# Far scores of the dilated heads read from copies sorted by residue

## The chip, the cores and the metric

The kernel runs on one core of a Trainium2 chip. The metric is the device time of one execution in microseconds (us). The kernel before takes 2331.02 us, the median of three runs (2330.0 to 2331.39).

## The reference, cut to what matters

The program is a trunk of two layers over 1024 positions and 1024 channels. Each layer projects its input into four groups of heads (Fourier mixing, grouped-query attention, a convolution module, dilated attention), joins them by an output projection, and then applies a two-matrix MLP; each half ends in a layer norm. What matters here is the dilated group, four heads of 64 channels:

```python
DIL_CONFIGS = ((128, 1), (512, 4), (2048, 16))      # window, dilation
def dilated_branch(q, k, v, dil, n, rel_bias):
    L = S // dil
    def to_res(t):                                   # positions sorted by their residue modulo dil
        return t.reshape(B, L, dil, H, hd).transpose(0, 2, 1, 3, 4).reshape(B * dil, L, H, hd)
    qr, kr, vr = to_res(q), to_res(k), to_res(v)
    ...
    s = jnp.einsum('bnqhd,bnkhd->bnhqk', qb, kw) * (hd ** -0.5)
    logits = jnp.where(valid, s + bias, NEG)         # |distance| <= n, T5 relative bias
    ...
```

Each query meets its neighbours at distance 1, those of its own residue modulo 4, and those of its own residue modulo 16. The branches are merged by their softmax denominators.

## The kernel before, in words

All matmuls run in a 32-bit format that keeps the upper part of a float, so values stand as a high and a low part; `split` (L168, L169) makes them, the high part on ScalarE and the difference on VectorE or GpSimd. `T` is one resident tile of 128 partitions x 8 rows x 2 parts x 1024 columns. It holds the layer's transposed activations and, during attention, pieces of other things. While attention runs, rows 0, 1, 4 and 5 hold the results of the Fourier and convolution groups, row 2 and the first half of row 3 hold the two `edge` tiles of the near branch (L629), row 6 takes the merged result of the first pair of dilated heads and row 7 that of the second pair, at its end. The second half of row 3 takes its first result near the end of attention.

`attention` handles 12 units: for each dilated head (4 to 7) a near unit and a far unit (class `Dilated`), then four dense heads (class `Dense`). A near unit is the branch of dilation 1; a far unit covers the branches of dilation 4 and 16 together, with one bias that counts both. Queries `qs` (high part in the upper, low part in the lower 64 partitions) and keys `kh`, `kl` (the same part twice) are loaded once for each head and used by its two units. Each of these tiles has two buffers, so the next head is loaded while this one runs.

A dilated unit has four steps. A step computes two score tiles of 128 queries x 256 keys, each as two matmuls, one with `kh` and one with `kl` (L823, L824): four matmuls per step. In a near step queries and keys are neighbours in memory. In a far step `i` queries and keys are those of residue `i` modulo 4, read at a stride of four elements:

```python
kk, q = slice(HD + i, HD + S, 4), me.q[:, 512 * qi + i:512 * qi + 512:4]
```

VectorE adds the bias and takes the row maximum (L834), ScalarE takes the exponential and its sum (L835). Seven steps later (`LAG`) TensorE transposes the probabilities (`turn`, L843), they are split, and two steps after that (`VLAG`) `values` multiplies by the values (L864); `join` (L677, L678) copies and adds the two halves of the result. `finish` and `merge` combine the near and the far unit of a pair of heads, by way of a round trip of the denominators through device memory (L890).

All of this is written into a table `todo` of step numbers, and the functions are called in the order of that table. Between the steps, sixteen pieces of the output projection for the other two groups (`others`, 12 matmuls each) are called. The order of the instructions on each engine is then set by a planner, which simulates the program with its own costs and may move instructions; the semaphores are made from what each instruction reads and writes. All loads and stores are issued by SP from one queue (L141); the two zero pads of the key tiles are written by GpSimd (L642, L643).

Of the kernel before, what the change touches and what calls it, by code (L numbers as in the profile page):

```python
# [15 lines left out]
F32 = mybir.dt.float32  # L16
# [6 lines left out]
P = 128  # L23
S = 1024
# [5 lines left out]
HD = 64  # L30
# [78 lines left out]
class Trunk:  # L109
# [513 lines left out]
    def attention(self, l, Wo):  # L623
        nc, tc = self.nc, self.tc
        g, v = nc.gpsimd, nc.vector
        with ExitStack() as c:
# [5 lines left out]
            for e in edge:  # L632
                for i in (1, 4):
                    v.memset(e[:, :, i].bitcast(F32), 0.0)
            pairs = {}

            def load_k(src, pad):
# [23 lines left out]
            def f4():  # L661
                return sm.tile([P, S], F32, tag="f4", name="f4", bufs=7)

            def s2():
                return self.sp.tile([P, S], F32, tag="s", name="s", bufs=2)
# [23 lines left out]
            class Dense:  # L689
# [22 lines left out]
                def scores(me, gr, kp):  # L712
                    t, n = 2 * gr + kp // 2, kp % 2
                    if n == 0:
                        me.s = s2()
                    s = me.s
                    q = me.q[:, t * P:(t + 1) * P]
                    nn = slice(n * 512, n * 512 + 512)
                    nc.tensor.matmul(s[:, nn], q, me.k[0][:, nn], start=True, stop=False)
                    nc.tensor.matmul(s[:, nn], q, me.k[1][:, nn], start=False, stop=True)  # L720
                    if n == 0:
                        return
                    pr = f4()
                    m = sm.tile([P, 2], F32, tag="m", name="m", bufs=4)
                    v.tensor_reduce(m[:, 0:1], s, AX.X, OP.max, negate=True)
                    nc.scalar.activation(pr, s, AF.Exp, bias=m[:, 0:1], scale=1.0, accum_out=m[:, 1:2])
                    v.reciprocal(me.rd[:, t, me.h % 2:me.h % 2 + 1], m[:, 1:2])
                    me.prob[t] = pr
# [34 lines left out]
            class Dilated:  # L763
# [5 lines left out]
                def load(me):  # L769
# [11 lines left out]
                    else:  # L781
                        me.st = pairs[me.near, me.h // 2].st

                def load_b(me):
                    b0 = self.bs[me.h - 4]

                    def skew(off, *dims):
                        return bass.AP(b0.tensor, b0.offset + off + P - 1, [[RL - 1, P], *dims])

                    if me.near:  # L790
                        me.b = sm.tile([P, 3, 256], F32, tag="ba", name="ba")
                        self.dma(me.b, skew(0, [0, 3], [1, 256]))
                        g.memset(me.b[:, 0, 0:HD], NEG)
                        g.memset(me.b[:, 2, 256 - HD:], NEG)
                    else:
                        me.b = sb.tile([P, 384], F32, tag="bb", name="bb")
                        self.dma(me.b, skew(LA, [1, 384]))
# [15 lines left out]
                def scores(me, i):  # L813
                    if i % 2 == 0:
                        me.s, me.p = s2(), f4()
                    sl = [slice((i % 2) * 512 + qi * 256, (i % 2) * 512 + qi * 256 + 256) for qi in range(2)]
                    for qi in range(2):
                        t = 2 * i + qi
                        if me.near:
                            kk, q = slice(t * P, t * P + 256), me.q[:, t * P:(t + 1) * P]  # L820
                        else:
                            kk, q = slice(HD + i, HD + S, 4), me.q[:, 512 * qi + i:512 * qi + 512:4]
                        nc.tensor.matmul(me.s[:, sl[qi]], q, me.k[0][:, kk], start=True, stop=False)  # L823
                        nc.tensor.matmul(me.s[:, sl[qi]], q, me.k[1][:, kk], start=False, stop=True)  # L824
                    for qi in range(2):
                        t = 2 * i + qi
                        pr = me.p[:, sl[qi]]
                        if me.near:
                            b = me.b[:, 0 if t == 0 else 2 if t == NT - 1 else 1]
                            st = me.st[:, t, :, me.h % 2]  # L830
                        else:
                            b = me.b[:, P * (1 - qi):P * (1 - qi) + 256]
                            st = me.st[:, 4 * qi + i, :, me.h % 2]
                        v.tensor_tensor_reduce(pr, me.s[:, sl[qi]], b, -1.0, 3e38, OP.add, OP.min, st[:, 0:1])  # L834
                        nc.scalar.activation(pr, pr, AF.Exp, bias=st[:, 0:1], scale=-1.0, accum_out=st[:, 1:2])  # L835
                    me.prob[i] = me.p[:, (i % 2) * 512:(i % 2) * 512 + 512].rearrange("p (q k n) -> p q k n", q=2, k=2)
# [76 lines left out]
            units = [Dilated(h, near) for h in range(4, 8) for near in (True, False)]  # L913
# [7 lines left out]
            first = {}  # L921
# [4 lines left out]
            def at(i, f, *args):  # L926
                todo.setdefault(i, []).append((f, args))
# [5 lines left out]
            for n, u in enumerate(units):  # L933
                hn = heads.index(u.h)
                at(0 if hn < 2 else begin[heads[hn - 1]], u.load)
                if isinstance(u, Dilated):
                    at(0 if n < 2 else first[units[n - 1]], u.load_b)
                at(0 if n < 2 else first[units[n - 1]] + LAG + VLAG + 1, u.load_v)
                last = first[u] + len(u.steps) + LAG + VLAG - 1
                at(last + 1, u.finish)  # L940
                if isinstance(u, Dilated):
                    at(last + 4, u.merge)
# [677 lines left out]
```

## Time and profile before

| | us |
|---|---|
| median of three runs | 2331.02 |
| the profiled execution | 2328.44 |
| its span, first to last instruction | 2326.3 |
| TensorE busy | 2217.1 (95%) |
| VectorE busy | 1776.1 (76%) |
| ScalarE busy | 1077.1 (46%) |
| GpSimd busy | 793.3 (34%) |

Times inside the trace count from the start of the span. A group of the profile is one line of the program on one engine with its operation and the shapes of its tiles; "idle before" is the time in which the engine stood in front of these instructions, and the arrow names what ended it. Matmuls overlap, so the distance of their starts tells what one costs, not its duration. `PEld` is the loading of the stationary operand (the queries, in the scores).

### The profile page before, as it was taken

How to read it: one execution, taken by the hardware profiler on the slowest of the kernel's cores; microseconds unless marked ns; L12 is line 12 of the kernel's file. 1: busy time of each engine (PE TensorE's matmuls, PEld its weight loads, DVE VectorE, ACT ScalarE, POOL GpSimd, SP SyncE). 2: the span in 40 equal slices, each digit the busy share in tenths (PEclk: the TensorE clock that was granted, in tenths of full speed). 3: DMA queues.
4: the chain of work that ended last, by engine and by line, in shares of the span. 5: the costliest groups of instructions: out<-in, count | busy, mean ns of one | idle time of the engine just before them, and what ended most of it. 6: DMA issues, size and time to landing. Idle time of an engine off the chain costs nothing. (4 is left out here: it accounts for less than half of the span.)

```text
span 2326.3 us, 31019 instructions
## 1 busy us (share of the span) xinstructions
PE 2217.1 (95%) x11212; PEld 1869.2 (80%) x11212; DVE 1776.1 (76%) x2500; ACT 1077.1 (46%) x1851; POOL 793.3 (34%) x540
## 2 busy tenths in 40 slices
PE   7999899998999999999989999999899999999997
PEld 6888887976778887888788798788677788788886
DVE  7687667968776777778957966788787767776699
ACT  3343767845333344333333446677443333443333
POOL 2361203016332233435514702110262333354353
PEclk9999999999999999999999999999999999999999
DMA  8444673043344467644223539621343444765433
GB/s 312 127 124 149 190 197 117 19 154 116 137 160 162 159 223 261 205 142 134 98 92 98 153 114 260 171 83 58 125 147 132 165 163 158 276 217 175 160 100 109
DMA packets 222950, 357.44 MB, mean 154 GB/s; under 512 B 21416, under 2 KB 100716, under 8 KB 221708
## 3 DMA queue, kind: packets, MB, share of 16 engines
q1 hardware_dynamic: 222796, 355.45, 47.1%
q8 instruction: 89, 1.46, 0.3%
q14 instruction: 65, 0.53, 0.1%
HBM read 244.44 MB, written 115.15 MB: 155 GB/s over the span
## 5 line engine op out<-in xcount | busy, mean ns | idle before, releaser
L174 PE MATMUL x<-T,w 128*128 128x512 f32 x1088 | 425.5, 393 | 12.2 <-DVE x L1441 4.7
L176 PE MATMUL x<-T,w 128*128 128x512 f32 x1088 | 425.0, 391 | 4.0 <-POOL w L169 2.6
L175 PE MATMUL x<-T,w 128*128 128x512 f32 x1088 | 426.2, 392 | 2.8 <-DVE T L169 2.8
L174 PEld LDWEIGHTS x<-T,w 128*128 128x128 f32 x1088 | 205.3, 189 | 60.8 <-issue 9.7
L176 PEld LDWEIGHTS x<-T,w 128*128 128x128 f32 x1088 | 205.6, 189 | 49.4 <-POOL w L169 3.4
L175 PEld LDWEIGHTS x<-T,w 128*128 128x128 f32 x1088 | 205.7, 189 | 46.7 <-DVE T L169 4.2
L1420 POOL TENSOR_TENSOR w<-w 128x512 fp32r<-128x512 f32 x76 | 147.5, 1961 | 225.1 <-ACT w L1418 225.1
L169 POOL TENSOR_TENSOR w<-raw,w 128x512 fp32r<-128x512 f32 x96 | 138.3, 1466 | 236.7 <-ACT w L168 221.4
L169 POOL TENSOR_TENSOR w<-s,w 128x512 fp32r<-128x512 f32 x68 | 104.3, 1544 | 246.2 <-ACT w L168 165.9
L174 PE MATMUL x<-E,w 128*128 128x512 f32 x384 | 150.6, 392 | 5.9 <-ACT h L1269 4.5
L176 PE MATMUL x<-E,w 128*128 128x512 f32 x384 | 150.1, 392 | 2.0 <-POOL w L169 1.8
L175 PE MATMUL x<-E,w 128*128 128x512 f32 x384 | 150.0, 391 | 0.0
L174 PE MATMUL s<-w,T 128*128 128x256 f32 (+1 forms) x432 | 137.0, 318 | 5.8 <-ACT T L168 5.4
L176 PE MATMUL s<-w,T 128*128 128x256 f32 (+1 forms) x432 | 135.0, 313 | 1.6 <-POOL T L169 1.2
L175 PE MATMUL s<-w,T 128*128 128x256 f32 (+1 forms) x432 | 134.8, 313 | 1.3 <-POOL w L169 1.3
L169 POOL TENSOR_TENSOR w<-rw,w 128x512 fp32r<-128x512 f32 x60 | 93.4, 1573 | 122.5 <-ACT w L168 122.5
L1047 DVE TENSOR_TENSOR s<-rw 128x512 f32<-128x512 f32 x62 | 53.4, 861 | 104.0 <-DMA rw<-in_w_ff_dram 103.7
L1418 ACT CAST w<-w 128x2048 fp32r<-128x2048 f32 x38 | 72.7, 1912 | 129.4 <-DMA w<-h_scratch 122.4
L174 PE MATMUL x<-T 128*128 128x512 f32 x320 | 126.1, 394 | 0.0
L175 PE MATMUL x<-T 128*128 128x512 f32 x320 | 125.5, 392 | 0.0
L176 PE MATMUL x<-T 128*128 128x512 f32 x320 | 125.4, 392 | 0.0
L456 DVE SCALAR_TENSOR_TENSOR o<-hp,cvT,o 128x1024 f32<-128x1024 f32 x88 | 113.3, 1287 | 2.4
(378 smaller groups left out, 5796.5 us busy)
## 6 DMA issues: line engine op xcount, KB each, us to landing
h_scratch<-h SPq DMA_DIRECT2D x224, 256.0 KB, 2.5
w<-h_scratch SPq DMA_DIRECT2D x38, 1024.0 KB, 5.4
rw<-in_w_ff_dram SPq DMA_DIRECT2D x64, 512.0 KB, 5.5
b<-in_w_ff_dram SPq DMA_DIRECT2D x24, 1024.0 KB, 5.5
raw<-x_scratch SPq DMA_DIRECT2D x72, 256.0 KB, 4.7
T<-h_scratch SPq DMA_DIRECT2D x18, 1024.0 KB, 5.3
raw<-in_w_in_dram SPq DMA_DIRECT2D x64, 256.0 KB, 3.5
rw<-in_w_ff_dram SPq DMA_DIRECT2D x10, 1024.0 KB, 5.3
```

Of the source, the lines that this page charges most:

```text
L169: (lo_eng or self.nc.vector).tensor_tensor(lo, src, hi.bitcast(F32), OP.subtract)
L174: mm(out, l[0], r[0], start=first, stop=False, skip_group_check=more)
L175: mm(out, l[0], r[1], start=False, stop=False, skip_group_check=more)
L176: mm(out, l[1], r[0], start=False, stop=last, skip_group_check=more)
L456: v.scalar_tensor_tensor(o, hp[:, m, k:k + S], cvT[:, m, k:k + 1], o, OP.mult, OP.add)
L1047: eng.tensor_tensor(quad(out), x, y, op)
L1418: nc.scalar.copy(A[:, :, 0], f32)
L1420: nc.gpsimd.tensor_tensor(A[:, j, 1], f32[:, j], A[:, j, 0].bitcast(F32), OP.subtract)
```

## The change

For each far unit a new function copies the head's queries and keys into rows of `T`, sorted by residue: `qr` is the second half of row 3 (1024 columns), `kr` is row 7, its two halves for the two parts of the keys. VectorE copies the queries, ScalarE the two parts of the keys. The copies are called at the step at which the near unit of the same head begins, ahead of its scores. The far scores then read 256 neighbouring columns of `kr` and 128 neighbouring columns of `qr`. There is one `kr` and one `qr` for all heads. The near scores read what they read before.

```diff
+            kr = self.T[:, 7]
+            qr = self.T[:, 2:4].rearrange("p k q n -> p (k q n)")[:, 24 * P:32 * P]
             pairs = {}
...
+                def by_residue(me):
+                    for copy, dst, x in ((v.tensor_copy, qr, me.q), (nc.scalar.copy, kr[:, 0], me.k[0][:, HD:HD + S]),
+                                         (nc.scalar.copy, kr[:, 1], me.k[1][:, HD:HD + S])):
+                        copy(dst.rearrange("p (r j) -> p r j", r=4),
+                             x.bitcast(F32).rearrange("p (j r) -> p r j", r=4))
+
...
                         if me.near:
-                            kk, q = slice(t * P, t * P + 256), me.q[:, t * P:(t + 1) * P]
+                            k, q = [x[:, t * P:t * P + 256] for x in me.k], me.q[:, t * P:(t + 1) * P]
                         else:
-                            kk, q = slice(HD + i, HD + S, 4), me.q[:, 512 * qi + i:512 * qi + 512:4]
-                        nc.tensor.matmul(me.s[:, sl[qi]], q, me.k[0][:, kk], start=True, stop=False)
-                        nc.tensor.matmul(me.s[:, sl[qi]], q, me.k[1][:, kk], start=False, stop=True)
+                            c = slice(256 * i, 256 * i + 256)
+                            k, q = [kr[:, x, c] for x in (0, 1)], qr[:, 256 * i + P * qi:256 * i + P * qi + P]
+                        nc.tensor.matmul(me.s[:, sl[qi]], q, k[0], start=True, stop=False)
+                        nc.tensor.matmul(me.s[:, sl[qi]], q, k[1], start=False, stop=True)
...
                     at(0 if n < 2 else first[units[n - 1]], u.load_b)
+                    if not u.near:
+                        at(first[units[n - 1]], u.by_residue)
```

## Rows read from the trace of the kernel before

**Rows 1.** The page, part 1: busy us, share of the span, instructions.
```profile
PE 2217.1 (95%) x11212; PEld 1869.2 (80%) x11212; DVE 1776.1 (76%) x2500; ACT 1077.1 (46%) x1851; POOL 793.3 (34%) x540
```

**Rows 2.** The windows view: both stages, their densest 30 us, 10 us of dense heads.
```profile
core 0: us, PE busy (x) PEld busy (x) DVE busy (x) ACT busy (x) POOL busy (x), PEclk, DMA share, GB/s
257.00:334.00 77.00, 71.22 (x384) 64.25 (x385) 46.18 (x180) 49.38 (x166) 6.70 (x25) 0.93 0.78 219
1404.00:1484.00 80.00, 73.90 (x415) 66.17 (x416) 54.11 (x195) 55.81 (x181) 6.76 (x26) 1.00 0.85 238
270.00:300.00 30.00, 29.23 (x163) 27.21 (x164) 20.93 (x87) 24.85 (x89) 3.67 (x16) 0.94 0.90 263
1420.00:1450.00 30.00, 29.89 (x170) 27.34 (x171) 22.21 (x85) 23.43 (x82) 2.93 (x15) 1.00 0.94 272
400.00:410.00 10.00, 10.00 (x73) 9.03 (x72) 9.76 (x17) 9.66 (x20) 1.29 (x1) 1.00 0.00 0
```

**Rows 3.** Time line of TensorE, layer 1: start, duration, line (us).
```profile
1440.76 0.28 PE L823 MATMUL s<-kh,qs 128*128 128x256 f32 x1
...
1441.23 0.28 PE L823 MATMUL s<-kh,qs 128*128 128x256 f32 x1
...
1442.98 0.36 PE L823 MATMUL s<-kh,qs 128*128 128x256 f32 x1
...
1443.53 0.49 PE L823 MATMUL s<-kh,qs 128*128 128x256 f32 x1
1443.84 0.42 PE L824 MATMUL s<-kl,qs 128*128 128x256 f32 x1
...
1444.55 0.66 PE L864 MATMUL o<-pT,vs 128*128 128x256 f32 x4
...
1445.40 0.58 PE L823 MATMUL s<-kh,qs 128*128 128x256 f32 x1
...
1446.51 0.42 PE L174 MATMUL tr<-w,T 128*128 128x512 f32 x1
```

**Rows 4.** Line 823 alone, near and far together: ns min/median/max.
```profile
L823 PEld LDWEIGHTS s<-kh,qs x128: 186/308/337, 257.1 to 1480.1; 128*128 128x128 f32 x128
```

**Rows 5.** Groups by form (ScalarE, VectorE), and line 907 alone (ns min/median/max).
```profile
L168 ACT CAST T<-d 128x1024 fp32r<-128x1024 f32 x16 | 16.8, 1051 | 63.7 <-DVE d L1471 42.0 <-PE x L176 21.7
L168 ACT CAST T<-b 128x2048 fp32r<-128x2048 f32 x30 | 57.2, 1908 | 81.6 <-PE x L176 78.1 <-DMA rw<-in_w_ff_dram 3.5
L598 ACT COPY u<-s 128x512 f32<-128x512 f32 x6 | 6.7, 1111 | 2.5 <-DVE T L169 1.5 <-PE s L176 1.0
L577 ACT COPY u<-s 128x512 f32<-128x512 f32 x3 | 1.8, 585 | 2.7 <-PE s L176 2.7
L169 DVE TENSOR_TENSOR T<-s,T 128x1024 fp32r<-128x1024 f32 x2 | 2.4, 1209 | 0.0
L907 DVE TENSOR_TENSOR y<-y,tr x12: 676/866/1082, 349.1 to 1540.9; 128x512 f32<-128x512 f32 x12
```

**Rows 6.** Time line of ScalarE: the first exponential of each layer.
```profile
261.76 0.51 ACT L835 ACTIVATE f<-f,std 128x256 f32<-128x256 f32 x1 [5.56 <-DVE std L834]
...
1407.85 0.51 ACT L835 ACTIVATE f<-f,std 128x256 f32<-128x256 f32 x1 [1.50 <-DVE std L834]
```

**Rows 7.** Time line of TensorE: the first dilated score of layer 0.
```profile
257.16 0.36 PE L823 MATMUL s<-kh,qs 128*128 128x256 f32 x1 [3.31 <-DMA kh<-k_scratch]
```

**Rows 8.** Waits, us in total, times, longest: the first three in layer 0, the others in layer 1.
```profile
POOL kh L642 <- PE s L823: 15.7, 2, 12.8
...
DVE w L890 <- DMA std<-merge_scratch: 5.1, 1, 5.1
...
SPq L141 <- PE s L824: 7.9, 3, 3.6
...
DVE w L890 <- DMA std<-merge_scratch: 3.4, 1, 3.4
...
SPq L141 <- PE s L824: 7.6, 4, 4.5
```

## The prediction

> **What bounds the kernel now.** The page comes first: TensorE is busy for 95% of the span, VectorE for 76%, ScalarE for 46% [rows 1]. These are averages, and the change touches only the stage in which the four dilated heads of a layer make their scores, so I cut that stage out with the windows view. It lasts from the first dilated score to the last one, 77 us in layer 0 (257 to 334) and 80 us in layer 1 (1404 to 1484). In it TensorE is busy for 71.2 and 73.9 us, ScalarE for 49.4 and 55.8, VectorE for 46.2 and 54.1, and the DMA engines carry a share of 0.78 and 0.85. In its densest 30 us TensorE is full (29.2 and 29.9), ScalarE is at 24.9 and 23.4, and the DMA share is 0.90 and 0.94 [rows 2]. So TensorE sets the pace here, with three others close behind it: what it is relieved of becomes time only as far as the others can follow.
>
> Then the matmuls themselves, in the time line of TensorE. A burst is the four matmuls of one score step. In a near burst the starts lie 0.12 us apart (four from 1440.76 to 1441.23); in a far burst, whose operands are read at a stride of four elements, 0.24 us apart (three from 1443.84 to 1444.55) [rows 3]. Its weight loads are longer too: the lines of the scores hold loads from 186 ns up to 337 ns, and the median over near and far is 308 ns [rows 4]. Both kinds have one shape and read the same tiles, so the stride alone is the difference, and copies without a stride should run like near bursts. That the change fails to do what it says is hardly possible.
>
> **What goes from TensorE.** Bursts are compared at the same place. Behind transposes a near burst holds the engine from 1442.98 to 1443.53, 0.55 us, a far one from 1445.40 to 1446.51, 1.11 us; behind other scores a near one takes 0.47 us (1440.76 to 1441.23) and a far one 1.02 us (1443.53 to 1444.55) [rows 3]. The gains are 0.56 and 0.55; between two far bursts the saving is four times 0.12, or 0.48. I take 0.53. There are 4 steps x 4 heads x 2 layers = 32 far bursts: 32 x 0.53 = 17.0 us, 8.5 in each layer (bounds 15.4 and 17.9). All of it lies on the engine that is full.
>
> **What ScalarE gets.** Two copies of 128x1024 per head, 16 in all, each reading every fourth element. No row shows ScalarE reading SBUF at a stride. From below: a 128x1024 cast with plain operands takes 1051 ns, and a stride will not make it shorter, so nothing below that. From above: a 128x512 copy from PSUM that *writes* at this stride takes 1111 ns, the plain one into the same tile 585 [rows 5]. That is 1.03 ns more for each element, so 1051 + 1024 x 1.03 = 2.1 us. I take the second kind, with the doubling that TensorE shows: the cast of 2048 elements takes 857 ns more than that of 1024, so 0.84 ns per element, and 1024 elements at twice that are 1908 ns. So 1.9 us a copy, 15.2 us per layer.
>
> The Trainium skill, page "SBUF — State Buffer", section Specifications, says that SBUF has lines of 16 bytes and that full bandwidth takes at least two hits in a line. A stride of four fp32 elements makes one hit per line; the far bursts at half rate agree. It speaks against this change, since the copies read the same way; by the rule they cost the 1.9 us, without it 1.05 us, and my forecast and my first rival differ in just this.
>
> Of these copies some are free. Head 4's come when ScalarE is idle: in layer 0 it waits 5.56 us for the first VectorE result, more than both copies, and in layer 1 1.50 us [rows 6]; the keys are there about then, since the first score itself waited for them until 257.16 [rows 7]. If that cover were gone it would cost 3.8 us a layer. What is left inside the stage is 6 x 1.9 = 11.4 us in layer 0 and, with some 1.1 us of head 4, 12.5 us in layer 1.
>
> **What VectorE gets.** One copy per head, 4 a layer. Nearest are the strided multiplies of the merge, at most 1082 ns against at least 676 for the plain ones of the same shape: 406 ns on 512 elements, or 0.81 us on 1024. A plain 128x1024 operation takes 1209 ns [rows 5]. So 2.0 us at the top; from below I allow half of the plain one, 0.6 us, since that reads two operands and the copy one. I take 2.0, 8 us a layer: 54.1 + 8 is 62.1 us in layer 1, below TensorE and ScalarE there. Cost: nothing, hidden beside TensorE's work; without that cover it would be 2 us for each of 6 head starts.
>
> **What the moves cost and give.** The copies of the next head overwrite rows that the far scores of this head read, so they wait for its last far burst, and they must end before the next far burst, 4 near steps later. In ScalarE's queue the casts of the transposes, the exponentials and the PSUM copies of the join stand behind them, and TensorE waits for the casts and joins to free PSUM. The order is the planner's, whose picture of the copies I do not know. In return the key tiles come free four steps earlier: SP waited 7.9 and 7.6 us for the last far scores before it could issue the next loads, and POOL 15.7 us in layer 0 [rows 8]. I count this at nothing, since TensorE waited for no key after each layer's first; gains up to 2 us are possible.
>
> **The sum.** How far can the stage shrink when ScalarE must also get through? It works for 49.4 + 11.4 = 60.8 us in layer 0 and 55.8 + 12.5 = 68.3 in layer 1. In its densest stretch here it was occupied 0.83 of the time (24.85 of 30); in the dense heads it reached 0.97 [rows 2]. I choose 0.87, near the former, since its queue is fed by the same mixture. Then the stage needs 60.8 / 0.87 = 69.9 us in layer 0, 7.1 less than 77, and 68.3 / 0.87 = 78.5 in layer 1, 1.5 less than 80; TensorE's 8.5 would have allowed more in both. Together -8.6 us. One wait takes some back: VectorE's first merge operation waited 5.1 us (3.4 in layer 1) for a round trip through memory [rows 8], which does not shrink with the work around it. About 2.5 far bursts lie between its issue and its use, 1.3 us, in each layer, so +2.6. The total is -6.0 us. The stages behind simply start earlier. The profiled execution took 2328.4 us (its span is 2326.3), so it would be 2322.4; the median of the runs shown is 2.6 us above the profiled one, so I forecast 2325.0 us.
>
> **Rivals.**
> *ScalarE reads a stride for free.* For it: TensorE takes an element every 0.46 ns (0.118 us for 256) and strided every 0.93, while ScalarE with 0.84 ns is slower than that anyway. Against it: the strided write of 1111 ns [rows 5]. The copies then add 6 x 1.05 = 6.3 us; at 0.87 ScalarE needs 64.0 and 71.4 us, TensorE 68.5 and 71.5, so TensorE binds and all is kept but the merge's wait: -17.0 + 2.6 = -14.4, 2316.6 us.
>
> *No gain.* ScalarE gets no more than the 0.83 of now: 73.3 us in layer 0 (-3.7) and 82.3 in layer 1 (+2.3), with the merge +1.2 in all; the key tiles' earlier release gives about that back. 2331 us.
>
> *Slower: a head start that TensorE stands through.* The two copies hold ScalarE's queue for 3.8 us, waiting as well for the last far burst, at each of the 6 head starts inside the stage. PSUM for transposes then stays full and TensorE stands. It decides from the point where a standstill is over 17.0 / 6 = 2.8 us; at the whole 3.8 the sum is 6 x 3.8 - 17.0 = +5.8, 2336.8 us. For it: ScalarE's queue is in order and already 0.83 full. Against it: seven steps of lag lie between scores and transposes, and the planner has matmuls of the output product to fill with.
>
> **How the numbers follow.** Forecast 0.40, free stride 0.20, no gain 0.18, slower 0.22. The measurement can tell 0.2% (4.7 us) from no change. Faster by more: most of the forecast (0.32), all of the free stride (0.20), 0.01 of no gain, 0.53. Slower by more: most of the last rival with a little of the others, 0.23. The rest, 0.24, is within. The range goes from 2314, where TensorE's 17 us are all kept, to 2337, the standstill; the forecast's own range is 2320 to 2328.
>
> **What would show it.** Far bursts with starts 0.12 us apart and weight loads near 186 ns (step 1). ScalarE's copies at 1.9 us; at 1.05 the first rival holds. VectorE's at 1 to 2 us. The stage in the windows view at some 70 and 78 us, with ScalarE above 0.85 of it. TensorE's waits at head starts on ScalarE's casts: short in the forecast, 3 us and more in the last rival. SP's and POOL's waits for far scores gone. I am wrong if the far bursts keep their spacing, or if the stage stays at 77 and 80 us while ScalarE is under 0.8.

## The result, and the profile after

The changed kernel takes 2349.57 us, the median of four runs (2344.19 to 2351.88), against 2330.51 for the kernel before, now the median of four runs as well: a ratio of 1.0086, with a 95% interval from 1.0064 to 1.0108. It is 19 us slower, and above the upper end of the forecast's range, 2337. Its profiled execution took 2344.19 us, 15.8 more than that of before, with a span of 2342.4.

The page, part 1, and then the changed far scores and the copies, each line alone (ns min/median/max, first and last start in us):

```profile
PE 2217.3 (95%) x11212; PEld 1863.6 (80%) x11212; DVE 1781.6 (76%) x2508; ACT 1106.0 (47%) x1867; POOL 795.2 (34%) x540
```

```profile
L834 PEld LDWEIGHTS s<-T x64: 186/188/337, 267.4 to 1496.8; 128*128 128x128 f32 x64
...
L791 DVE CAST T<-qs x8: 1073/1109/2124, 254.6 to 1473.3; 128x1024 fp32r<-128x1024 f32 x8
L791 ACT CAST T<-kl x8: 2012/2050/2093, 259.2 to 1475.2; 128x1024 fp32r<-128x1024 f32 x8
```

The weight loads of the far scores fall to a median of 188 ns, where near and far together had 308 [rows 4], and TensorE is as busy as before all the same [rows 1]. Now the stages, in the windows view. The first two rows answer to [rows 2]; the last two are cut from the layer's first dilated score to its first dense score, which moves from kernel to kernel:

```profile
core 0: us, PE busy (x) PEld busy (x) DVE busy (x) ACT busy (x) POOL busy (x), PEclk, DMA share, GB/s
257.00:334.00 77.00, 62.48 (x346) 54.21 (x347) 47.14 (x170) 62.13 (x161) 6.61 (x25) 0.89 0.79 209
1404.00:1484.00 80.00, 67.71 (x353) 55.44 (x352) 49.42 (x170) 64.34 (x161) 10.90 (x34) 0.91 0.82 227
257.40:339.30 81.90, 67.78 (x376) 58.76 (x377) 50.56 (x182) 66.12 (x175) 6.61 (x25) 0.90 0.80 212
1409.50:1493.00 83.50, 70.67 (x376) 58.14 (x377) 52.46 (x184) 65.64 (x175) 6.68 (x25) 0.92 0.83 228
```

The same cut in the kernel before:

```profile
257.20:332.60 75.40, 69.78 (x376) 63.00 (x377) 44.83 (x177) 48.89 (x165) 6.70 (x25) 0.93 0.79 220
1404.10:1476.10 72.00, 66.36 (x377) 59.80 (x378) 48.74 (x179) 51.51 (x167) 6.66 (x26) 1.00 0.87 243
```

The stages grew by 6.5 and 11.5 us, 18.0 together, so the whole loss lies in them (the profiled execution grew by 15.8). TensorE, once full, now stands idle for 14.1 us (81.90 - 67.78) and 12.8, where it stood 5.6 in each. And its granted clock is lower: in layer 1 it was 1.00, and 0.92 now. How the two go together is seen around 1470 us in layer 1: VectorE's time line, TensorE's, and the windows view of the same place.

```profile
1470.45 0.18 DVE L901 TENSOR_TENSOR w<-std 128x16 f32<-128x16 f32 x1 [4.05 <-DMA std<-merge_scratch]
1470.55 0.42 DVE L845 CUSTOM_DVE_ANT_0 f<-s,bb 128x256 f32<-128x256 f32 x1
```

```profile
1471.37 0.38 PE L834 MATMUL s<-T 128*128 128x256 f32 x1 [4.04 <-DVE std L845]
1471.60 0.28 PE L835 MATMUL s<-T 128*128 128x256 f32 x1
1471.71 0.28 PE L834 MATMUL s<-T 128*128 128x256 f32 x1
...
1478.00 0.41 PE L834 MATMUL s<-kh,qs 128*128 128x256 f32 x1
1478.22 0.41 PE L835 MATMUL s<-kl,qs 128*128 128x256 f32 x1
1478.43 0.41 PE L834 MATMUL s<-kh,qs 128*128 128x256 f32 x1
```

```profile
1467.00:1472.00 5.00, 0.96 (x8) 0.63 (x5) 1.51 (x9) 0.97 (x4) 0.16 (x2) 1.00 0.68 146
1472.00:1479.00 7.00, 6.02 (x24) 4.98 (x24) 5.23 (x20) 7.00 (x15) 0.00 (x0) 0.51 0.45 139
1479.00:1484.00 5.00, 4.92 (x30) 4.00 (x29) 4.01 (x16) 4.88 (x17) 0.00 (x0) 1.00 0.13 41
```

VectorE stands 4.05 us before the merge, which waits for its round trip. The score work queued behind it (L845) comes late, TensorE waits 4.04 us for its PSUM, and in the 7 us after that pause the granted clock is 0.51, the lower level, 1.2 GHz: matmuls of 256 columns then start 0.21 to 0.22 us apart instead of 0.11 to 0.12. So this late load is paid for twice. It is no single case: of the four longest pauses of TensorE inside the two stages, three (2.5, 2.8 and this one) come with a stretch at 0.5 of the clock that begins before their end or within 2 us of it; behind the fourth (2.6 us) one begins only 6 us later. The waits view of layer 0's stage shows what else VectorE stood for (us, times, longest):

```profile
DVE f L845 <- POOL ba L803: 7.2, 3, 3.2
...
DVE w L901 <- DMA std<-merge_scratch: 4.6, 1, 4.6
```

These are the near bias tile, of which there is one buffer (GpSimd writes its two edges behind the load), and the merge. Both waits were there before, 5.8 us for the bias tile and 5.1 for the merge [rows 8]. What is new is that TensorE waits behind VectorE. First the view of before, in layer 0, then that of the changed kernel, in layer 0 and in layer 1:

```profile
DVE f L834 <- POOL ba L793: 5.8, 2, 3.8
...
PE s L823 <- DVE std L834: 1.1, 2, 0.7
```

```profile
PE s L834 <- DVE std L845: 7.2, 8, 2.8
```

```profile
PE s L834 <- DVE std L845: 6.1, 5, 4.0
```

In layer 1 the kernel before has no such wait in its stage.

### The profile page after: what moved, and what is told of

Its sections match the earlier page's. It is cut to its first block, busy times and chain, and to the rows that moved or that the text cites. A ratio compares the mean times of both kernels' runs of the same rounds, so it can differ in the third digit from the quotient of the medians.

```text
span 2342.4 us, 31072 instructions
## 1 busy us (share of the span) xinstructions
PE 2217.3 (95%) x11212; PEld 1863.6 (80%) x11212; DVE 1781.6 (76%) x2508; ACT 1106.0 (47%) x1867; POOL 795.2 (34%) x540
```

## Experiments

**First four: ScalarE's queue or the planner's order?** Theory Q: the copies fill ScalarE's queue and the stage follows it. Rival O: the planner, which weighs the copies by its own costs, gave every engine a new order, and that and the loads that it moves cost the time. All ratios are against the kernel before, which ran again with each batch of runs; its median went from 2326.2 to 2330.5 us, so ratios are compared, and times only within one batch.

*e3*: the key copies read neighbours (1.04 us instead of 2.05); the keys then stand in the wrong order. All engines keep the order of the changed kernel.

```diff
-    x.bitcast(F32).rearrange("p (j r) -> p r j", r=4))
+    x.bitcast(F32).rearrange("p (j r) -> p r j" if dst is qr else "p (r j) -> p r j", r=4))
```

> The changed kernel with the same instructions in the same order on every engine; only ScalarE's key copies read neighbouring elements instead of every fourth (the keys then stand in kr unsorted, so the far scores are those of other keys). Each of the 16 copies should fall from 2.05 us to 1.05 us. Theory Q (ScalarE's queue: the copies stand in front of exponentials, casts and joins): most of the 16 us come back, 2332 to 2338 us. Rival O (the order that the planner made with the copies in it, and the loads it moved, is what costs): within 4 us of the changed kernel, 2345 to 2352.

2350.39 us, 1.0083 [1.0060, 1.0107]. Half of the copies' work gone, nothing gained: Q falls.

*e8*: the far scores read the copies at a stride of four, in the same order again.

```diff
-    k, q = [kr[:, x, c] for x in (0, 1)], qr[:, 256 * i + P * qi:256 * i + P * qi + P]
+    k, q = [kr[:, x, i:S:4] for x in (0, 1)], qr[:, 512 * qi + i:512 * qi + 512:4]
```

> The changed kernel in the same order on every engine, copies as they are, but the far scores read kr and qr at a stride of four (so they pair elements of other residues). It takes back what TensorE gained and nothing else: 32 bursts of 0.5 us, 17 us. If TensorE still sets the pace in the stages, 2360 us or more; if ScalarE does (Q) or waits for loads do, less than half of it shows, 2350 to 2357 us.

2354.31 us, 1.0104 [1.0080, 1.0128]. The 17 us of TensorE are worth some 4 here, less than the intervals can tell.

*e2*: only head 4 is copied, and heads 5 to 7 read its copies; 18 of 24 copies are left out.

```diff
-    if not u.near:
+    if not u.near and u.h == 4:
```

> Only head 4 is copied; heads 5 to 7 read head 4's copies (so their far scores are head 4's). 12 of 16 ScalarE copies and 6 of 8 VectorE copies are gone, TensorE's gain stays. Q: 2316 to 2324 us, the 17 us of TensorE nearly whole. O: the order is a new one, and nothing says it is better: 2325 to 2345 us.

2338.36 us, 1.0034 [1.0017, 1.0051]: cheap reads, a quarter of the copies, and still slower. The planner had made another order for it. *e4*: `v.tensor_copy` for all three copies, so ScalarE has none.

> All three copies of a head on VectorE, where the query copy took 1.1 us: 3.3 us per head on VectorE, none on ScalarE. Q: ScalarE is as before, TensorE's gain counts, VectorE's new load costs some of it: 2322 to 2332 us. If a block of over 3 us on either engine at the head start is what costs, 2340 us or more.

2342.59 us, 1.0051 [1.0032, 1.0070]. The order had changed again. So work and order had to be taken apart.

**Order and work apart.** In the next runs the order is not left to the planner. The order of each engine's instructions, as the planner made it for one of the two kernels, is held by scheduling edges without semaphores:

```diff
+    for e, runs in order.items():
+        l = by[e] if e != "SP" else [i for i in by[e] if "DMA" in type(i).__name__]
+        want = [l[s + k] for s, n in runs for k in range(n)]
...
+        for a, b in zip(want, want[1:]):
+            tc.add_manual_dep(b, a.name, how, reason="order")
```

The profiles show each engine's instructions in the order that was asked for. No run holds the kernel before in its own order with nothing else changed; but the changed kernel's order, held (e12 below, 1.0090) and as the planner leaves it (e3, 1.0083), gives times that agree. In the order of before the copies have no place, and the planner sets in only them. *e9* is the changed kernel in that order:

> The changed kernel, with all its 24 copies and its reads of neighbouring columns, but with every other instruction of all five queues held in the order that it has in the kernel before; only the copies are set in by the planner. Theory O (the loss is the planner's new order and the loads that it moves, not the copies): the time falls below the kernel before, 2318 to 2331 us, since the far bursts are 17 us shorter on TensorE and the copies cost what the first forecast gave them. Rival W (the copies themselves and the new waits that their data impose cost the time, in whatever order): 2343 us or more, as the changed kernel (2349.6).

2337.58 us, 1.0040 [1.0025, 1.0054]: between the two theories' figures. The order is worth about half of the loss, and the rest is the work. Its trace (of an execution of 2343.72 us, among the longer ones) shows how, in layer 1, on ScalarE, VectorE and TensorE:

```profile
1449.89 2.04 ACT L791 CAST T<-kh 128x1024 fp32r<-128x1024 f32 x1
1451.84 2.09 ACT L791 CAST T<-kl 128x1024 fp32r<-128x1024 f32 x1
...
1455.92 0.37 ACT L681 COPY y<-o 64x256 f32<-64x256 f32 x1
```

```profile
1456.32 0.41 DVE L682 TENSOR_TENSOR y<-y,o 64x256 f32<-64x256 f32 x1 [3.28 <-ACT y L681]
```

```profile
1457.57 0.36 PE L834 MATMUL s<-T 128*128 128x256 f32 x1 [3.03 <-DVE std L845]
```

Two copies in a row hold ScalarE for 4 us, the join's copy, behind them and four exponentials, comes late, VectorE stands 3.28 us for it, and TensorE 3.03 behind VectorE.

> The kernel before, without any copy, its far scores at a stride of four, but with its instructions on TensorE, VectorE and ScalarE held in the order that they have in the changed kernel; the loads (SP) and GpSimd keep the order of the kernel before. Theory O, if the order on the engines is what costs: 2338 to 2352 us. O, if it is the order of the loads alone: 2331 us, within 4. Rival W: 2331 us, within 4.

*e10*, the old work: 2344.38 us, 1.0073 [1.0053, 1.0093], as O had it: the new order on three engines costs 17 us without any copy.

> The changed kernel in its own order on TensorE, VectorE and ScalarE, with the queues of SP (all loads and stores) and GpSimd held in the order of the kernel before. If the loss is that earlier key loads stand in front of the bias tile's load: VectorE's 13 us of waits for the bias in layer 0 go, and the time falls to 2330 to 2340 us. If it is the order on the engines, or the copies: 2344 to 2352 us.

*e11*, SP and GpSimd in the old order: 2345.20 us, 1.0074 [1.0052, 1.0096]. The order of the loads alone is not it. *e12*:

```diff
-                        copy(dst.rearrange("p (r j) -> p r j", r=4),
-                             x.bitcast(F32).rearrange("p (j r) -> p r j", r=4))
+                        copy(dst[:, 0:S:256], x.bitcast(F32)[:, 0:4])
```

> The changed kernel in its own order on all five queues, copies included, but each copy moves 4 of its 1024 columns (the far scores read what else lies in these rows of T), so nearly all of the copies' work is left out while every order, wait and read stays. Theory O: 2340 to 2350 us, still slower than before, since the copies' work was not what cost. Rival W: with some 45 us of ScalarE and VectorE work gone and the far bursts 17 us shorter, 2314 to 2328 us.

2350.64 us, 1.0090 [1.0068, 1.0112]: in the changed kernel's order the copies' work costs nothing that can be told.

**The same ladder in the order of before**, with the edits of e12, e3 and e4, and for e15 `g.tensor_copy` for the keys. Theory C: here ScalarE's copies cost. Rival V: VectorE and ScalarE set the pace anyway.

> As e9 (the changed kernel's work in the order of the kernel before on all five queues), but each copy moves 4 of its 1024 columns (the far scores read what else lies in these rows of T): the shorter far bursts alone, nearly without the copies' work. Theory C (in the order of before it is ScalarE's strided copies, up to 4.1 us in one piece, that hold back what TensorE waits for): the time falls below the kernel before, 2312 to 2322 us. Rival V (VectorE and ScalarE set the pace of the stage, so a faster TensorE only stands more and gets a lower clock): no gain, 2326 to 2336 us.

*e13*, 4-column copies: 2319.73 us, 0.9972 [0.9961, 0.9984]: faster. This is what the cheap reads are worth, 6.5 us.

> As e9, but ScalarE's key copies read neighbouring elements (1.04 us instead of 2.05; the keys then stand in the wrong order). Theory C: half of the way from e9 to e13, 2322 to 2331 us. Rival V: as e9, 2333 to 2342 us.

*e14*, plain key copies: 2324.96 us, 0.9991 [0.9980, 1.0001].

> As e9, but GpSimd makes the two key copies, so that ScalarE has none. GpSimd is idle in two thirds of the stage and no run has shown its price for such a copy, so the copies may come late or slow VectorE. Theory C, if GpSimd takes at most 3 us for one: 2315 to 2328 us, faster than before. Rival V: 2333 to 2342 us as e9. If GpSimd takes 5 us or more for one: the first far unit waits, 2340 us or more.

*e15*, key copies on GpSimd: 2328.22 us, 1.0007 [0.9996, 1.0017]. GpSimd takes 2.1 to 2.5 us for one, but the time is just above C's figures and not below the kernel before. (Its room in the stage is larger than the expectation has it: it is busy for 6.7 of 77 us [rows 2].)

> As e9, but VectorE makes all three copies at 1.1 us each. Theory C: ScalarE is free and VectorE has 2.2 us more for each head, so 2320 to 2331 us. Rival V: VectorE sets the pace and has 18 us more to do, so 2336 us or more.

*e16*, all copies on VectorE: 2330.25 us, 1.0016 [1.0002, 1.0029]. C holds in three of the four runs, and V in none: 4 columns 0.9972, plain 0.9991, strided 1.0040 (e9). The copies cost some 16 us in this order (0.0068 of 2330), of which the stride on ScalarE alone is 11 (e9 against e14, which hold their copies at the same places); in the changed kernel's order they cost none. In e13 the planner also set VectorE's six later copies four or five instructions earlier than in e9, so its 16 us are not the copies' length alone. The stages of e12 and e13, the same work in the two orders, by the windows view:

```profile
258.20:341.00 82.80, 69.31 (x377) 61.31 (x378) 47.14 (x182) 51.83 (x175) 6.65 (x25) 0.86 0.79 211
1417.70:1498.90 81.20, 68.78 (x377) 58.25 (x378) 47.51 (x182) 51.98 (x175) 6.66 (x25) 0.89 0.89 231
```

```profile
255.80:328.60 72.80, 64.46 (x376) 56.97 (x377) 47.86 (x182) 52.04 (x175) 6.65 (x25) 0.91 0.88 237
1400.20:1471.30 71.10, 62.59 (x377) 54.36 (x377) 48.88 (x182) 52.19 (x175) 6.54 (x25) 0.95 0.87 246
```

VectorE and ScalarE are busy for nearly the same time, and the stages take 164.0 against 143.9 us: 20.1 of the 28.5 us by which the two profiled executions differ.

**Is it the waits for loads?** Theory D: in the new order VectorE's queue comes too early to work that waits for a load. Rival E: the engines wait for one another. The loads are still made, but nothing reads them; the bias and the merge's second branch are left out of the result.

```diff
-    b = me.b[:, 0 if t == 0 else 2 if t == NT - 1 else 1]
+    b = self.T[:, 0, 0, 0:256].bitcast(F32)
...
-    m2, d2 = me.s2[:, :, 0], me.s2[:, :, 1]
+    m2, d2 = me.st[:, :, 0], me.st[:, :, 1]
```

> The kernel before in its own order, but VectorE never waits for a load there: the scores add two pieces of row 0 of T in place of the bias tiles, and the merge takes the far unit's denominators as they stand; the loads and the round trip are still made, and nothing reads them. It is the base line for e18. Theory D (the new order costs because VectorE's queue reaches work that waits for a load too early): before has such waits too, 3.8 + 2.0 + 5.1 us in layer 0 and 1.6 + 3.4 in layer 1, so 2312 to 2328 us. Rival E (the order costs through TensorE, ScalarE and VectorE waiting for one another): 2324 to 2331 us.

*e17*: 2318.31 us, 0.9956 [0.9940, 0.9972]. VectorE's waits for loads cost the kernel before some 10 us, as D had it and E had not.

> e10 (the work of the kernel before, engines in the order of the changed kernel) with the edit of e17. Theory D: the 17 us between e10 and before shrink to less than 6 between this and e17, so 2314 to 2330 us. Rival E: they stay, 2336 to 2348 us.

*e18*: 2341.35 us, 1.0040 [1.0026, 1.0055]: 23 us above e17. D falls by it, but TensorE's time line in layer 1 shows a wait of another kind:

```profile
1457.10 0.36 PE L823 MATMUL s<-kh,qs 128*128 128x256 f32 x1 [4.06 <-DMA kh<-k_scratch]
...
1459.66 0.55 PE L824 MATMUL s<-kl,qs 128*128 128x256 f32 x1 [2.20 <-DMA kl<-k_scratch]
```

The new order was made for keys that come early, since the copies free their tiles; with the old work they come late. So e18 charges the order with up to 7 us too much: in layer 1 its scores wait 8.5 us for keys, those of the other kernels 1.2 or 1.3. In e10 they wait 1.2, so e10 stands. e12 against e13, where the work is the changed kernel's, is the cleaner pair.

> The changed kernel, copies, order and all, with the edit of e17. Theory D: as the waits for loads go, the copies on ScalarE come to bear as in e9, so 2325 to 2338 us. Rival E: 2342 to 2351 us, as the changed kernel.

*e19*: 2342.84 us, 1.0052 [1.0037, 1.0066], 8 us below the changed kernel, and at the lower end of E's figures.

*e20*: the edit divides the copies.

```diff
-                    for copy, dst, x in ((v.tensor_copy, qr, me.q), (nc.scalar.copy, kr[:, 0], me.k[0][:, HD:HD + S]),
+                    for copy, dst, x in ((v.tensor_copy, qr, me.q), (v.tensor_copy, kr[:, 0], me.k[0][:, HD:HD + S]),
...
```

> As e9 (the changed kernel's work in the order of before), with the queries and the high keys copied by VectorE and the low keys by ScalarE: one ScalarE copy of 2.05 us for each head instead of two in a row, one VectorE copy of 1.1 us more. From e9 (+9 us) and e16 (+4 us): between them and the 6.5 us that e13 shows as the most, 2320 to 2332 us. Below 2324 us it would beat both kernels.

2324.32 us, 0.9982 [0.9969, 0.9996]. It leaves nothing out and is faster than both kernels, than the one before by about 4 us (0.0018 of 2330), with an interval that ends just under 1. Its stages:

```profile
257.70:329.90 72.20, 63.45 (x376) 55.04 (x377) 55.59 (x186) 58.63 (x171) 7.47 (x25) 0.95 0.85 237
1405.80:1474.70 68.90, 60.45 (x376) 52.18 (x377) 55.58 (x187) 58.83 (x171) 7.14 (x25) 1.00 0.88 251
```

VectorE and ScalarE share the load evenly, and in layer 1 the clock never falls. Whether the shorter piece on ScalarE or the smaller load there is what helps, e20 doesn't tell.

**The clean pair without the load waits** (edits of e12 and e17):

> e12 (order of the changed kernel, each copy 4 columns) with the edit of e17 (bias from row 0 of T, merge without its round trip). Theory F (the order costs through waits for loads; the copies on ScalarE cost as much only where those waits are gone): within 6 us of e22, 2312 to 2324 us. Rival G (the order costs through the engines waiting for one another): 2332 us or more, 12 or more above e22.

*e21*: 2330.21 us, 0.9999 [0.9981, 1.0017].

> e13 (order of before, each copy 4 columns) with the edit of e17: the base line for e21 and the floor of the stage with TensorE's short bursts. From e13 (-6.5 us) and e17 (-11.8 us): 2306 to 2318 us under both theories.

*e22*: 2314.12 us, 0.9927 [0.9902, 0.9953]. Theory F (waits for loads after all) falls, and G's distance holds, though e21 itself lies a little below G's 2332: 16 us stay between the two (2330.21 - 2314.12), where e12 and e13 have some 27 (1.0090 - 0.9972, of 2330). So VectorE's waits for loads are some 11 us of the order's price, an estimate that the four intervals leave open by several us, and the larger part is not theirs. Of the 16 us the two profiles show 8.4 in the stages (140.9 against 132.5); the rest is spread over parts of the program where kernels of one order differ by as much among themselves. What makes these 16 us stays open, and so does which engine's order it is: e10 and e11 point at TensorE, VectorE and ScalarE together, since the queues of SP and GpSimd are in the old order there.

| work | order of the changed kernel | order of before |
|---|---|---|
| copies as changed | 1.0086 | 1.0040 (e9) |
| plain key copies | 1.0083 (e3) | 0.9991 (e14) |
| 4-column copies | 1.0090 (e12) | 0.9972 (e13) |
| the same, no load waits | 0.9999 (e21) | 0.9927 (e22) |
| copies as changed, no load waits | 1.0052 (e19) | not run |

The left column shows how the two costs of the changed kernel hide each other: with the waits for loads the copies' work costs nothing (1.0086, 1.0090), without them 0.0053, some 12 us (1.0052, 0.9999).

## Why the prediction was wrong

**TensorE's 17 us**: the mechanism was right. Far bursts start 0.11 to 0.12 us apart, as near ones. Their worth was not: even with nearly free copies and the old order they give 6.5 us (e13). VectorE, ScalarE and the DMA engines stood close behind TensorE [rows 2]: with its bursts shorter it pauses more, and behind most of the long pauses comes a stretch at the lower clock, for which the sum had no term. In e13's two stages TensorE's busy time falls by 9.1 us against before, not by 17, its idle time grows by 5.6, and the granted clock is 0.91 and 0.95 where it was 0.93 and 1.00.

**ScalarE's copies**: 1.9 us each forecast, 2.05 measured, and the bound of 2.1 held. The Trainium skill ("SBUF — State Buffer", Specifications) has lines of 16 bytes, of which full bandwidth wants two hits. ScalarE agrees with it, 2.05 us strided against 1.04 plain. For VectorE nothing here speaks for or against it: its strided copy takes 1.11 us, and no run has a plain one of its own to set beside that.

The conversion into time failed: for the change in the old order the forecast of -6.0 us stands against some +9 (e9). Two steps of it were wrong. The first is the cover of head 4's copies, which were counted as free in layer 0 and nearly so in layer 1. ScalarE was idle there, but the copies could not use the time: the first starts at 259.22 us, after a wait of 5.5 us, and they then stand in front of the first exponential, which starts at 265.41 where before it started at 261.76 [rows 6]:

```profile
259.22 2.04 ACT L791 CAST T<-kl 128x1024 fp32r<-128x1024 f32 x1 [5.51 <-DVE T L169]
...
265.41 0.51 ACT L846 ACTIVATE f<-f,std 128x256 f32<-128x256 f32 x1
```

The second is the windows. They were called first to last dilated score, but the last one of layer 0 starts at 336.8, and both reach into the dense heads, which begin at 332.6 and 1476.1. The share of 0.87 itself was not far off, as the stages of e9 show:

```profile
257.20:333.50 76.30, 66.06 (x376) 57.49 (x377) 51.72 (x182) 66.38 (x175) 6.67 (x25) 0.91 0.77 217
1411.10:1490.30 79.20, 66.15 (x377) 57.09 (x378) 52.44 (x183) 66.28 (x175) 6.71 (x25) 0.91 0.77 221
```

ScalarE's share is 66.4 of 76.3 us, or 0.87, and 66.3 of 79.2, or 0.84. With the stages cut at the first dense score and all eight copies of 2.05 us in each, the same rule gives (48.9 + 16.4) / 0.87 = 75.1 us and (51.5 + 16.4) / 0.87 = 78.0, so 0.3 less and 6.0 more than before, and +8 with the merge's 2.6: about what e9 shows. The slower rival, with a chance of 0.22, comes out near it too, at +5.8 us for two copies in one piece with TensorE standing behind, and e9's trace has one such standstill of 3.0 us; which of the two sums is the right one the runs don't tell.

**VectorE's copy**: 1.1 us, inside 0.6 to 2.0; one of the eight took 2.12 (the last section says why).

**The moves and the order**: in the kernel as it ran, this is the step that failed. It said "The order is the planner's, whose picture of the copies I do not know" and counted it at nothing, with gains up to 2 us possible. It costs 11 us with the copies as they are (1.0086 against 1.0040), some 27 with nearly free ones, and in that order the copies' own work hides behind the waits for loads (e19 and e21): that is why e3 and e12 gained nothing. No rival of the prediction had the order in it. That the slower rival's sign came true is therefore in part luck. The forecast also had SP's and GpSimd's waits for far scores gone [rows 8]. GpSimd's went. SP's did not: its waits view in the two stages of the changed kernel still has 6.0 us in layer 0 and 9.0 in layer 1.

```profile
SPq L141 <- PE s L834: 3.5, 2, 2.1
...
SPq L141 <- PE s L835: 2.5, 1, 2.5
```

```profile
SPq L141 <- PE s L834: 8.4, 2, 6.3
...
SPq L141 <- PE s L835: 0.6, 2, 0.4
```

**The merge**: 2.6 us for its round trip was the right kind of cost. VectorE waits 4.6 and 4.05 us for it in the changed kernel, 5.1 and 3.4 before, so the wait grew by 0.2 in all; but in layer 1 TensorE now pays 4.04 us for it and then the clock.

## What to carry to other kernels

Where a planner sets the order, an added instruction changes more than its own cost: price an edit in the old order and in the new one, by holding the order, before blaming the instruction. An engine that is full while others stand close behind may give back little of what it is relieved of (here 6.5 of 17 us), and where its pauses lower the granted clock, less still. An idle stretch is no cover for new work that has to wait through it as well. Divide added copies between the engines that have room: here that was the only complete form of the change that gained (e20).

## What the runs showed of the hardware that was not expected

VectorE copies 128x1024 fp32 elements at a stride of four in 1.11 us, less than a plain two-operand pass over as many (1.21 [rows 5]), while ScalarE's copy doubles with the stride; what a plain copy takes on VectorE no run shows. GpSimd takes 2.07 to 2.5 us for the same copy, and in that kernel (e15) VectorE's query copy has a median of 2.08 us instead of 1.11:

```profile
L791 DVE CAST T<-qs x8: 1081/2082/2249, 255.4 to 1460.2; 128x1024 fp32r<-128x1024 f32 x8
L791 POOL CAST T<-kl x8: 2027/2498/2983, 262.0 to 1461.4; 128x1024 fp32r<-128x1024 f32 x8
L791 POOL CAST T<-kh x8: 2012/2070/2084, 264.5 to 1459.4; 128x1024 fp32r<-128x1024 f32 x8
```

The traces show that the two engines hold each other up. In the changed kernel seven of VectorE's eight copies take 1.07 to 1.13 us, and the one of 2.12 us starts just behind a subtraction of GpSimd:

```profile
1407.33 1.29 POOL L169 TENSOR_TENSOR w<-raw,w 128x512 fp32r<-128x512 f32 x1
...
1407.45 2.12 DVE L791 CAST T<-qs 128x1024 fp32r<-128x1024 f32 x1 [2.91 <-DMA qs<-q_scratch]
```

The two overlap for 1.17 us, and the copy is 1.0 us longer than the others. In e9 two copies start under such a subtraction: with 0.53 us of it to go one takes 1.50 us, with 1.10 to go the other takes 2.06. In e16, beside constants that GpSimd writes, VectorE's copies take their 1.05 to 1.09 us, but the constant that otherwise takes 0.15 us takes 2.2.
